# A product-key expert layer on one core: 640 dense and 384 gathered tokens instead of 704 and 320, and the second expert product turned round

## The chip, the cores and the metric

The kernel runs as one program on one core of a Trainium2 chip. The metric is the device time of one execution in microseconds (us). Three timed runs of the kernel before gave 2978.72, 2979.86 and 2987.46 us; their median, 2979.86 us, is what the change is compared with. Engines are named as in the profile: PE is TensorE, with PEld for its weight loads, DVE is VectorE, ACT is ScalarE, POOL is GpSimd and SP is SyncE. "Stage" below means a stretch of the program that is named by its place in time.

## The reference, cut to what matters

A sequence of 1024 tokens of width 1024 goes through a token-mixing half (norm, projections, a gated recurrence, a short convolution, an output projection, residual) and then through the half that the change touches, a layer of 16384 single-neuron experts (PEER):

```python
s = jnp.einsum('thpk,hpnk->thpn', q, sub_keys)          # 8 heads x 2 halves x 128 keys
top_s, top_i = lax.top_k(s, 16)
best_s, best_pos = lax.top_k(cand_s.reshape(T, 8, 256), 16)
gate = jax.nn.softmax(best_s, axis=-1)
u = expert_u[idx]                                        # 128 chosen experts of each token
v = expert_v[idx]
act = jax.nn.gelu(jnp.einsum('td,thkd->thk', xb, u))
return jnp.einsum('thk,thkd->td', gate * act, v)
```

After it come a gated residual and a final RMS norm. All is float32; the kernel reaches that precision on PE by splitting each operand into a high and a low part of fp32r and taking three products (high-high, high-low, low-high).

## The kernel before

**Two ways for the experts.** The tokens are divided. For the last `TD` = 704 ("dense") tokens the kernel computes all 16384 experts, in 128 blocks of 128: the first product (activations of a block for all dense tokens, `u_steps`, line L1161, 24 matmuls of 384 and 24 of 320 columns a block), a gelu, a multiplication with the block's gates, which are zero where an expert was not chosen (`w_step`, L1376), and the second product with the block's rows of v (`v_phase`, L1395). For the first `REST` = 320 ("gathered") tokens it fetches the 128 chosen rows of u and of v of each token by indirect DMA from POOL (L1082) and works on them on DVE: one multiply-and-sum per row of u (L1100) and one multiply-add per row of v (L1092). One such step handles one row for each of 128 tokens, a transfer of 128 x 4 KB. Two tiles of 128 tokens take 128 steps each, the half tile of 64 tokens takes 64 steps, with half of each token's experts on either half of the partitions and a small product that folds them: 320 steps of a row of u and a row of v.

**The stages in time.** Up to about 350 us: modulation, norm 1 and the mixing of the first half of the sequence. 350 to 420: queries and scores of the gathered tokens. 420 to 690: mixing of the second half, output projection, norm 2. 690 to 838: queries, scores and first top-k of the dense tokens (`query`, L873; `top16`, L922 to L926). 838 to 980: second top-k and index picking for the dense tokens. 980 to 1256: the dense gates (`gates`), for a group of 64 tokens at a time: DVE builds one-hot products (L1312, L1318), PE multiplies them (L1327), ACT copies the result (L1330), and SP stores 4 MB of gates in pieces of 512 bytes (L1335). 1256 to 2960: the main loop over 128 blocks. After that the end: transposing, residual, final norm, store.

**What runs beside it.** Forty blocks' activations (`EARLIES`) are computed ahead (`u_early`), strewn over the second top-k and the gates, and wait in DRAM (`ged`). The work on the gathered tokens is a generator, `background()`: top-k of each tile, then the rows. `advance(cost)` moves it on by a number of VectorE microseconds; the stages call it at rates of their own (`RATES`): 0.15 in the second mixing, 0.1 in the two stages of the dense top-k ("E"), 0.0 in the gates ("F"), 0.5 for the early blocks that remain after them ("G"), and evenly in the main loop, so that it ends at 97% of TensorE's columns (`along`, `per_column`). A planner orders the instructions of each engine: one whose inputs are ready can be put ahead of earlier program order. The row operations L1100 and L1092 are exempt from that (`keep_in_program_order`): each stands behind what was traced on DVE just before it. Rows are received in four buffers (`ROWS`) and one more. SP issues the loads of u (`wl`), of v (`vl`), of gates (`gsb`) and of early blocks, and the stores, in one queue; POOL issues the gathers in another.

**The second product.** Blocks are taken in groups of `SB` = 3. For each of the two column groups of tokens and each of eight slices of 128 output columns, v's slice is stationary and the weighted activations W (128 experts by 384 or 320 tokens) move: 9 matmuls into one PSUM bank. Two of the 16 results stay in PSUM for the whole loop (`FIXED`); the other 14 are added to accumulators in SBUF by DVE (L1411). The results are transposed, so the end of the kernel turns them back with 96 small products (L1424, L1425) before the final norm.

Of the kernel before, what the change touches and what calls it, by code (L numbers as in the profile page):

```python
# [32 lines left out]
TD = 704  # L33
REST = S - TD
SPL = [(0, 384), (384, TD - 384)]
# [4 lines left out]
# the gathered tokens of the last, half tile get their experts together with the half tile of the others  # L40
FULL = REST // P
LAST = REST % P
assert LAST and LAST == P - TD % P
SB = 3
# [18 lines left out]
FIXED = [(0, 0), (1, 0)]  # L63
# [17 lines left out]
RF = 0.0  # L81
# [16 lines left out]
def build(tc, A, out, dbg=None):  # L98
# [27 lines left out]
    def rsqrt(r, v, tmp, e=0):  # L126
        """of v / 4 ** e: a first guess from the exponent, then Newton steps"""
# [12 lines left out]
    with root:  # L140
# [6 lines left out]
        qgd = scratch.tile([16, P, LAST], F32, name="qgd")  # L147
# [29 lines left out]
        # ---------------------------------------------------------------- stationary operands  # L177
        # all of [P, KC, P], in the order in which TensorE takes them; each is fetched two and split one ahead
# [24 lines left out]
        def halve(n):  # L203
            """there is a third set of halves at times"""
# [7 lines left out]
        def deepen(pl, first, n, every):  # L212
            """that many more from the first on: one of so many goes into a pool of its own"""
# [18 lines left out]
        def ahead():  # L232
            """in the midst of the products with one: split the next"""
# [5 lines left out]
        # ---------------------------------------------------------------- constants, modulation  # L239
# [4 lines left out]
        # three buffers of four row tiles, in turn of the normalised input or w_out, and of the mix or the residual  # L244
# [36 lines left out]
        # TensorE gets to its full clock while the first loads are under way  # L281
# [29 lines left out]
        def mod_part(sec, wa, d):  # L311
            """some columns of a section of the modulation"""
# [5 lines left out]
        def mod_part_rows(sec, wa, d):  # L318
            """the same on TensorE, as a row that is turned into columns"""
# [28 lines left out]
        # ---------------------------------------------------------------- norm 1 and the values  # L348
# [14 lines left out]
        def lnT1(xs, pl, k, h1, onact=False):  # L363
            """transpose a column block of the four row tiles, scale, shift and split it"""
# [16 lines left out]
        def wi_load(pl, k, lb=3, hb=2, ahead=0, wait=[]):  # L381
            """loads run ahead of the splits"""
# [34 lines left out]
        # ---------------------------------------------------------------- projections, token mixing  # L417
# [6 lines left out]
        # lower bounds  # L424
# [16 lines left out]
        # a window of 32 columns of it holds ones in one of them  # L441
# [12 lines left out]
        def mixing(half, mods, h1, og):  # L454
            """projections, recurrence, convolution and group norms of half a sequence, into og"""
# [43 lines left out]
            # blocks of w_in: per head f, q, g (0..11), per conv group c, x, b (12..23)  # L499
# [54 lines left out]
            # masks of the levels: the highest bit in which s and t differ, for s < t  # L554
# [117 lines left out]
            def finish(g):  # L672
                """the scales of a group, from the rows of all of them"""
# [18 lines left out]
        # ---------------------------------------------------------------- w_out, norm 2  # L692
# [169 lines left out]
        def query(pl, hp, hs, spl, tiles, new_pq, new_sc, sink, n):  # L862
# [3 lines left out]
            if n > TD:  # L866
                SY.dma_start(qT[:, TD:], qgd[hp])
# [665 lines left out]
```

## Time and profile before

| | before |
|---|---|
| median of three timed runs | 2979.86 us |
| span of the profiled execution | 2982.4 us |
| PE busy | 2902.0 us (97%) |
| PE weight loads busy | 2750.8 us (92%) |
| DVE busy | 2524.2 us (85%) |
| ACT busy | 946.0 us (32%) |
| POOL busy | 796.2 us (27%) |
| moved by DMA | 709.65 MB, 238 GB/s over the span |

The profile is of one execution, whose first to last instruction took 2982.4 us. No other duration of that execution is on record; its span lies 2.5 us above the median of the timed runs and within their range. A busy share is an average over stages with different limits, so the windows by stage say more than the table. PE's busy time is modelled from pipelined matmuls: the time from one start to the next is what a matmul costs, not its listed duration. DVE's listed durations overlap in the same way by some 80 ns.

### The profile page before, as it was taken

The numbers are of one execution on the slowest core, as the hardware profiler recorded it, in microseconds if no ns is written. First come the engines' busy times: TensorE is split into PE (matmuls) and PEld (weight loads), VectorE is DVE, ScalarE is ACT, GpSimd is POOL, SyncE is SP. The second block draws the span as 40 slices with busy tenths as digits, with TensorE's granted clock in tenths as the row PEclk, the third lists the DMA queues.
The fourth block names the chain that finished last, engine by engine and source line by source line (L and its number), as shares of the span: only waits on it lengthen the run. The fifth ranks groups of instructions, "written<-read, shape, count | busy, mean of one in ns | idle before, by whom it ended". The sixth has DMA issues, their size and how long they took to land.

```text
span 2982.4 us, 47131 instructions
## 1 busy us (share of the span) xinstructions
PE 2902.0 (97%) x18242; PEld 2750.8 (92%) x18242; DVE 2524.2 (85%) x5314; ACT 946.0 (32%) x1541; POOL 796.2 (27%) x661
## 2 busy tenths in 40 slices
PE   8999999999999999999999999999999999999998
PEld 6887888878999899999999999999999999999997
DVE  6885559988999877568889989889989988989987
ACT  5643655433122444422222222222222221222221
POOL 0000000000000000015454445435545444444450
PEclk8999999989999999999999999999999999999999
DMA  7424342244223577778889888889889888889883
GB/s 269 146 88 142 130 142 71 85 146 147 61 89 108 181 238 241 234 257 299 302 305 335 314 309 327 320 304 336 304 306 325 319 317 318 307 318 332 304 311 128
DMA packets 286898, 709.65 MB, mean 238 GB/s; under 512 B 26513, under 2 KB 124817, under 8 KB 284370
## 3 DMA queue, kind: packets, MB, share of 16 engines
q1 hardware_dynamic: 192994, 365.56, 35.5%
q0 software_dynamic: 93680, 341.09, 32.2%
q8 instruction: 142, 2.33, 0.3%
q14 instruction: 82, 0.67, 0.1%
HBM read 633.65 MB, written 72.88 MB: 237 GB/s over the span
## 4 chain that ended last, share of the span: by engine, by line
PE 64%; DVE 17%; DMA 10%; issue 5%; ACT 2%; POOL 1%; SPq 0%; DVEq 0%; ACTq 0%; POOLq 0%
PE pv L1395 22%; PE pa L1161 19%; PE pp L467 6%; DMA wl<-in_uT 5%; PE pq L873 4%; PE pacc L1395 3%; DVE wl L114 2%; DMA Wl<-ged 2%; PE ps L577 1%; PE pp L873 1%; PE pg L1327 1%; PE pp L378 1%; DVE gacc L1092 1%; PE pp L714 1%; DVE acc L1411 1%
## 5 line engine op out<-in xcount | busy, mean ns | idle before, releaser
L1161 PE MATMUL pa<-h2h,wh 128*128 128x384 f32 (+1 forms) x1840 | 598.4, 325 | 2.7 <-ACT ge L1166 2.6
L1161 PE MATMUL pa<-h2h,wl 128*128 128x384 f32 (+1 forms) x1840 | 593.9, 323 | 0.0
L1161 PE MATMUL pa<-h2l,wh 128*128 128x384 f32 (+1 forms) x1840 | 593.7, 323 | 0.0
L1395 PE MATMUL pv<-Wh,vh 128*128 128x384 f32 (+1 forms) x1792 | 580.6, 324 | 11.7 <-DVE acc L1411 11.1
L1395 PE MATMUL pv<-Wl,vh 128*128 128x384 f32 (+1 forms) x1792 | 577.3, 322 | 0.0
L1395 PE MATMUL pv<-Wh,vl 128*128 128x384 f32 (+1 forms) x1792 | 577.0, 322 | 0.0
L1395 PEld LDWEIGHTS pv<-Wh,vh 128*128 128x128 f32 x1792 | 336.9, 188 | 22.4 <-DVE acc L1411 19.6
L1161 PEld LDWEIGHTS pa<-h2h,wh 128*128 128x128 f32 x1840 | 346.0, 188 | 4.5 <-ACT ge L1166 3.8
L1161 PEld LDWEIGHTS pa<-h2l,wh 128*128 128x128 f32 x1840 | 346.2, 188 | 0.0
L1161 PEld LDWEIGHTS pa<-h2h,wl 128*128 128x128 f32 x1840 | 346.0, 188 | 0.3 <-DVE wl L114 0.3
L113 ACT ACTIVATE Wh<-Wl 128x704 fp32r<-128x704 f32 x128 | 101.6, 793 | 747.8 <-PE pv L1395 588.2
L1395 PEld LDWEIGHTS pv<-Wh,vl 128*128 128x128 f32 x1792 | 337.0, 188 | 0.0
L1395 PEld LDWEIGHTS pv<-Wl,vh 128*128 128x128 f32 x1792 | 336.9, 188 | 0.0
L113 ACT ACTIVATE wh<-wl 128x1024 fp32r<-128x1024 f32 x187 | 198.0, 1059 | 420.8 <-DMA wl<-in_uT 205.2
L114 DVE TENSOR_TENSOR wl<-wl,wh 128x1024 fp32r<-128x1024 f32 x187 | 227.8, 1218 | 97.7 <-ACT wh L113 95.9
L1411 DVE TENSOR_TENSOR acc<-acc,pv 128x320 f32<-128x320 f32 (+1 forms) x574 | 286.1, 513 | 11.6 <-PE pv L1395 11.3
L114 DVE TENSOR_TENSOR vl<-vl,vh 128x1024 fp32r<-128x1024 f32 x128 | 156.0, 1219 | 18.3 <-ACT vh L113 18.2
L113 ACT ACTIVATE vh<-vl 128x1024 fp32r<-128x1024 f32 x128 | 134.6, 1052 | 79.5 <-DMA vl<-in_v 45.4
L467 PE MATMUL pp<-h1h,wh 128*128 128x512 f32 x384 | 156.6, 408 | 0.0
L467 PE MATMUL pp<-h1h,wl 128*128 128x512 f32 x384 | 152.5, 397 | 3.5 <-DVE wl L114 3.4
L1376 DVE TENSOR_TENSOR Wl<-Wl,gsb 128x704 f32<-128x704 f32 x128 | 113.2, 885 | 48.4 <-DMA Wl<-ged 36.9
L467 PE MATMUL pp<-h1l,wh 128*128 128x512 f32 x384 | 152.3, 397 | 0.0
(1778 smaller groups left out, 5978.2 us busy)
## 6 DMA issues: line engine op xcount, KB each, us to landing
wl<-in_uT SPq DMA_DIRECT2D x128, 512.0 KB
vl<-in_v SPq DMA_DIRECT2D x128, 512.0 KB
gd<-stg SPq DMA_DIRECT2D x11, 4096.0 KB
gsb<-gd SPq DMA_DIRECT2D x64, 704.0 KB
wl<-in_win SPq DMA_DIRECT2D x48, 512.0 KB
wa<-in_wada SPq DMA_DIRECT2D x16, 1024.0 KB
wl<-in_wq SPq DMA_DIRECT2D x32, 512.0 KB
ged<-ge SPq DMA_DIRECT2D x40, 352.0 KB
```

The lines of the kernel that those rows point to most:

```text
L113: C.activation(hi, src, AF.Copy)
L114: V.tensor_tensor(lo, src, hi.bitcast(F32), op=OP.subtract)
L378: T.matmul(pvs[t], l[:, t * P:(t + 1) * P], r, start=(k == 0 and l is h1[0][k] and r is wi[0]), stop=(k == KC - 1 and l is h1[1][k]))
L467: T.matmul(pp, l[:, k], r[k], start=(i == 0), stop=(i == 3 * KC - 1))
L577: T.matmul(ps_[:, c], X[:, cs_], Y[:, cs_], start=True, stop=True)
L714: T.matmul(pm, l[:, t * P:(t + 1) * P], r, start=(k == 0 and l is yh[k] and r is woh[k]), stop=(k == KC - 1 and l is yl[k]))
L873: T.matmul(pq[:, :m], l[:, k], hs[k, r][:, o:o + m], start=(i == 0), stop=(i == 3 * KC - 1))
L1092: V.scalar_tensor_tensor(ac, r, aw[:, j:j + 1], ac, op0=OP.mult, op1=OP.add))
L1161: T.matmul(pa[:, :n], l[:, k], h2[k, r][:, o:o + n], start=(i == 0), stop=(i == 3 * KC - 1))
L1376: V.tensor_tensor(gv, gv, gs[b // GB][:, :, b % GB], op=OP.mult)
L1395: T.matmul(pv[:, :n], l[:, c * P:(c + 1) * P], r[:, o:o + n], start=(i == 0 and (not fx or b0 == 0)), stop=(i == 3 * (b1 - b0) - 1 and (no ...
L1411: V.tensor_tensor(a, a, pv[:, :n], op=OP.add)
```

## The change

The dense tokens become 640 (five full tiles instead of five and a half) and the gathered ones 384 (three full tiles), so that the half tile, its fold and its round trip through DRAM are gone. The first product has two column groups of 320. The gates have ten groups of 64 tokens instead of eleven. In the second product the roles are exchanged: W's 128 tokens are stationary, 512 columns of v move, and the result of a tile of 128 tokens is 128 x 1024 in two PSUM banks, in token rows. Groups are of four blocks. One tile's sum stays in PSUM; the other four are added to SBUF accumulators of 128 x 1024. The end needs no transposing: a multiplication with a row of gate2, an addition and the norm. The background's rate in the gates goes from 0.0 to 0.9. The scores of the gathered tokens are stored two at a time instead of four. Comments are taken out as well.

```diff
-TD = 704
+TD = 640
-SPL = [(0, 384), (384, TD - 384)]
+SPL = [(0, 320), (320, 320)]
-SB = 3
+SB = 4
-FIXED = [(0, 0), (1, 0)]
+FIXED = 0
-RF = 0.0
+RF = 0.9
...
-        accs = {(j, c): mp.tile([P, n], F32, name=f"acc{j}{c}") for j, (_, n) in enumerate(SPL) for c in range(KC)
-                if (j, c) not in FIXED}
-        fixed = {f: psM.tile([P, 512], F32, name=f"pacc{f[0]}{f[1]}", bufs=1) for f in FIXED}
+        accs = {t: mp.tile([P, DM], F32, name=f"acc{t}") for t in range(DT) if t != FIXED}
+        fixed = psM.tile([P, DM], F32, name="pacc", bufs=1)
-        work = 3.0 * KC * TD * (2 * NK - len(EARLIES)) * SPREAD
+        work = 3.0 * (KC * TD * (NK - len(EARLIES)) + DM * DT * NK) * SPREAD
...
         def v_phase(b0, b1):
             last = b1 == NK
-            for j, (o, n) in enumerate(SPL):
-                for c in range(KC):
-                    fx = (j, c) in fixed
-                    pv = fixed[j, c] if fx else new_pv()
+            for t in range(DT):
+                fx = t == FIXED
+                pv = fixed if fx else psM.tile([P, DM], F32, name="pv", bufs=2)
+                for j in range(2):
                     i = 0
                     for b in range(b0, b1):
                         wh, wl = Ws[b]
                         vh, vl = Vs[b]
-                        for l, r in ((vh, wh), (vl, wh), (vh, wl)):
-                            T.matmul(pv[:, :n], l[:, c * P:(c + 1) * P], r[:, o:o + n],
+                        for l, r in ((wh, vh), (wh, vl), (wl, vh)):
+                            T.matmul(pv[:, j * 512:(j + 1) * 512], l[:, t * P:(t + 1) * P], r[:, j * 512:(j + 1) * 512],
...
+                    if not last:
+                        along(3.0 * (b1 - b0) * 512)
+                if last:
+                    a = x1s[t] if fx else accs[t]
+                    V.tensor_tensor(rs[t], pv, g2, op=OP.mult)
+                    V.tensor_tensor(rs[t], rs[t], a, op=OP.add)
+                    norm_store(mp, REST + t * P, P, [rs[t][:, :512], rs[t][:, 512:]], fw, rs[t], sq)
+                elif not fx:
+                    a = accs[t]
+                    if b0 == 0:
+                        V.tensor_copy(a, pv)
                     else:
-                        V.tensor_tensor(a, a, pv[:, :n], op=OP.add)
...
+                        V.tensor_tensor(a, a, pv, op=OP.add)
```

## Rows read from the trace of the kernel before

**Rows 1.** The page of the profile: the span, the busy times of two engines, the chain of waits by engine, and the two DMA queues (packets, MB, time of their packets as a share of 16 engines' span; q0 is POOL's queue, q1 SP's).

```profile
span 2982.4 us, 47131 instructions
PE 2902.0 (97%) x18242; PEld 2750.8 (92%) x18242; DVE 2524.2 (85%) x5314; ACT 946.0 (32%) x1541; POOL 796.2 (27%) x661
...
q1 hardware_dynamic: 192994, 365.56, 35.5%
q0 software_dynamic: 93680, 341.09, 32.2%
...
PE 64%; DVE 17%; DMA 10%; issue 5%; ACT 2%; POOL 1%; SPq 0%; DVEq 0%; ACTq 0%; POOLq 0%
```

**Rows 2.** Busy time of each engine by stage. Columns: stretch, its length, busy us (instructions) of PE, PEld, DVE, ACT and POOL, the granted TensorE clock, the mean busy share of the 16 DMA engines, GB/s.

```profile
350.00:420.00 70.00, 67.53 (x462) 65.19 (x461) 23.43 (x25) 31.67 (x73) 1.59 (x3) 1.00 0.51 167
420.00:690.00 270.00, 251.83 (x1278) 207.00 (x1278) 247.33 (x852) 126.47 (x215) 9.47 (x11) 0.95 0.32 107
690.00:838.00 148.00, 148.00 (x970) 146.76 (x969) 138.60 (x749) 31.62 (x55) 0.00 (x0) 1.00 0.27 90
838.00:980.00 142.00, 133.81 (x807) 130.58 (x806) 138.04 (x611) 36.77 (x56) 0.76 (x1) 0.98 0.31 103
980.00:1256.00 276.00, 265.51 (x2486) 248.44 (x2487) 212.53 (x366) 136.16 (x254) 0.00 (x0) 0.99 0.74 226
1256.00:1283.00 27.00, 26.22 (x165) 25.88 (x164) 4.55 (x5) 6.04 (x9) 0.00 (x0) 1.00 0.95 312
1283.00:2960.00 1677.00, 1663.07 (x10300) 1649.33 (x10298) 1495.01 (x2129) 392.98 (x549) 781.08 (x634) 1.00 0.85 307
2960.00:2983.00 23.00, 13.38 (x97) 10.25 (x96) 13.32 (x49) 4.12 (x12) 0.00 (x0) 0.82 0.29 107
```

**Rows 3.** The same view of the steady part of the main loop alone.

```profile
1300.00:2900.00 1600.00, 1587.42 (x9841) 1576.90 (x9840) 1434.60 (x2012) 370.99 (x509) 773.21 (x628) 1.00 0.87 314
```

**Rows 4.** The chain of waits in order of time: start, us, what, and how many matmuls in a row. The L1395 pieces are of 320 columns (9.24) and of 384 (10.92), L1161 alternates 24 of each, L467 has 512 columns.

```profile
99.42 5.58 PE pp L467 x24
...
1021.32 18.62 DMA wl<-in_uT
...
1315.34 15.40 PE pa L1161 x96
...
1344.56 9.24 PE pv L1395 x63
...
1370.80 10.92 PE pv L1395 x63
```

**Rows 5.** The first product (L1161) alone by stretch: length, busy us (matmuls) of PE and (weight loads) of PEld, clock, DMA. A block has 48 matmuls.

```profile
838.00:980.00 142.00, 132.66 (x792) 129.22 (x792) 0.98 0.31 103
980.00:1256.00 276.00, 197.39 (x1063) 169.73 (x1064) 0.99 0.74 226
1256.00:2960.00 1704.00, 695.20 (x4291) 689.38 (x4289) 1.00 0.86 307
```

**Rows 6.** Waits in the main loop (1283 to 2960 us): who waited for whom, us in total, times, longest.

```profile
POOL more L1082 <- DVE gacc L1092: 76.9, 53, 9.6
...
PEld pv L1395 <- DVE acc L1411: 19.6, 30, 2.4
...
DVE more L1100 <- DMA more<-in_u,idx: 7.1, 4, 2.9
```

**Rows 7.** Instructions of DVE in order of time, in the main loop: start, us, what. Successive starts show what each costs when they follow one another.

```profile
1703.19 1.28 DVE L1092 SCALAR_TENSOR_TENSOR gacc<-grow__17319,aw,gacc 128x1024 f32<-128x1024 f32 x1
1704.38 0.48 DVE L1411 TENSOR_TENSOR acc<-acc,pv 128x320 f32<-128x320 f32 x1
...
1705.61 1.22 DVE L1100 SCALAR_TENSOR_TENSOR grow__17344<-grow__17344,hx 128x1024 f32<-128x1024 f32 x1
...
1706.75 0.48 DVE L1411 TENSOR_TENSOR acc<-acc,pv 128x320 f32<-128x320 f32 x1
1707.15 0.18 DVE L1109 TENSOR_TENSOR aw<-aw,gkg 128x32 f32<-128x32 f32 x1
...
1710.39 0.88 DVE L114 TENSOR_TENSOR Wl<-Wl,Wh 128x704 fp32r<-128x704 f32 x1
1711.19 1.22 DVE L114 TENSOR_TENSOR vl<-vl,vh 128x1024 fp32r<-128x1024 f32 x1
1712.33 1.28 DVE L1092 SCALAR_TENSOR_TENSOR gacc<-grow__17429,aw,gacc 128x1024 f32<-128x1024 f32 x1
```

**Rows 8.** Groups of instructions with their shapes: count, busy us, mean ns, idle before. The two forms of L1411 in the main loop, and the gates' matmul from 980 to 1256 us.

```profile
L1411 DVE TENSOR_TENSOR acc<-acc,pv 128x384 f32<-128x384 f32 x287 | 153.0, 545 | 0.2 <-PE pv L1395 0.2
L1411 DVE TENSOR_TENSOR acc<-acc,pv 128x320 f32<-128x320 f32 x287 | 133.2, 480 | 11.5 <-PE pv L1395 11.1
L1327 PE MATMUL pg<-O,P 128*128 128x128 f16 x1408 | 101.7, 219 | 9.9 <-DVE P L1318 9.4
```

**Rows 9.** One of the five operations of the top-k (L922) by stretch: length, busy us (instructions) of DVE, clock, DMA. A tile of 128 tokens has 24. The first two stretches are of gathered tiles.

```profile
420.00:545.00 125.00, 5.97 (x24) 0.99 0.25 82
545.00:650.00 105.00, 5.75 (x24) 0.92 0.33 109
650.00:690.00 40.00, 0.00 (x0) 0.89 0.50 177
690.00:900.00 210.00, 36.14 (x144) 0.98 0.27 91
```

More of the change, by code (lines that the diff above doesn't have):

```diff
@@ L41 @@
 FULL = REST // P
-LAST = REST % P
-assert LAST and LAST == P - TD % P
-SB = 3
+assert REST % P == 0 and TD % P == 0
+SB = 4
 GB = 2
@@ L890, in query @@
             scores.append(score)
-            return qT
         keysT = [None]
@@ L902, in sink_gather @@
         def sink_gather(hp, g, w, sc):
-            if hp % 4 == 0 and g == 0:
-                sgs[0] = qg.tile([P, FULL, 4, P], F32, name="sg", bufs=2)
+            if hp % 2 == 0 and g == 0:
+                sgs[0] = qg.tile([P, FULL, 2, P], F32, name="sg", bufs=2)
             s_ = sgs[0]
-            C.activation(s_[:w, g, hp % 4], sc, AF.Copy)
-            if hp % 4 == 3:
+            C.activation(s_[:w, g, hp % 2], sc, AF.Copy)
+            if hp % 2:
                 o = GG[g][0]
-                SY.dma_start(scd[o:o + w, hp - 3:hp + 1], s_[:w, g])
+                SY.dma_start(scd[o:o + w, hp - 1:hp + 1], s_[:w, g])
         for hp in range(16):
-            qT = query(qg, hp, hg2, [(0, REST)], GG[:FULL], lambda: bank("pp"), lambda: bank("ps"), sink_gather, REST)
-            SY.dma_start(qgd[hp], qT[:, FULL * P:])
+            query(qg, hp, hg2, [(0, REST)], GG, lambda: bank("pp"), lambda: bank("ps"), sink_gather, REST)
         scores.pop()()
@@ L1110, in background @@
                 parts = [ac[:, :512], ac[:, 512:]]
-                if c_ > 1:
-                    fold = gp.tile([P, P], F32, name="fold", bufs=1)[:, :w]
-                    V.tensor_copy(fold, ident[:, :w])
-                    for c in range(1, c_):
-                        V.tensor_tensor(fold, fold, ident[:, c * w:(c + 1) * w], op=OP.add)
-                    for j in range(2):
-                        pf = foldps[0]()[:w]
-                        T.matmul(pf, fold, parts[j], start=True, stop=True)
-                        parts[j] = pf
                 x1 = gp.tile([P, DM], F32, name="hx", bufs=1)
@@ L1204, in sink_dense @@
             top16(qp, sc, P, ts[:w, t, hp], ti[:w, t, hp])
-        foldps[0] = lambda: psE.tile([P, 512], F32, name="pq", bufs=3)
         for hp in range(16):
@@ L1236, in build @@
             early_along(pick(new, [a[:, t] for a in ab], ti[:, t], [i1[:, t], i2[:, t]]))
-        lo_, hi_ = slice(0, LAST), slice(P - LAST, P)
-        n = steps[FULL]
-        sl = slice(sum(steps[:FULL]), sum(steps))
-        i1f, i2f, gkf = (a[hi_, DT - 1].rearrange("p k h -> p (k h)") for a in (i1, i2, gk))
-        ih = qp.tile([P, P], I32, name="ih")[hi_]
-        V.scalar_tensor_tensor(ih, i1f, float(NK), i2f, op0=OP.mult, op1=OP.add)
-        SY.dma_start(idx[lo_, sl], ih[:, :n])
-        SY.dma_start(gkg[lo_, sl], gkf[:, :n])
-        V.tensor_copy(idx[hi_, sl], ih[:, n:])
-        V.tensor_copy(gkg[hi_, sl], gkf[:, n:])
         stE.close()
@@ L1456, in build @@
             prev += SB
-        fw = grow() if NG else mp.tile([P, DM], F32, name="fw")
+        fw, g2 = grow(), grow()
         SY.dma_start(fw, bcast_rows(A["fnw"]))
+        SY.dma_start(g2, bcast_rows(g2d[0]))
         sq = mp.tile([P, DM], F32R, name="vh", bufs=SLOTS)[:, :512].bitcast(F32)
@@ L1462, in build @@
         for t in range(DT):
-            n = ("wl", "wh")[t % 2] if t < 5 else "vl"
-            x1 = (mp.tile([P, DM], F32R, name=n, bufs=VS) if n == "vl" else
-                  up.tile([P, KC, P], F32R, name=n, bufs={"wl": WL, "wh": 2}[n]))
-            x1 = (x1 if n == "vl" else x1.rearrange("p k e -> p (k e)")).bitcast(F32)
-            SY.dma_start(x1[:WT[t]], x1d[REST + t * P:REST + t * P + WT[t]])
-            x1s.append(x1)
-            if t < 3 and NG:
-                rs.append(grow())
-            elif t < 5 and NG:
-                rs.append(gp.tile([P, DM], F32, name=("hx", "gacc")[t - 3], bufs=1))
-            else:
-                rs.append(mp.tile([P, DM], F32R, name="vl", bufs=VS).bitcast(F32))
-        for c in range(KC):
-            for j, (o, n) in enumerate(SPL):
-                if (j, c) not in fixed:
-                    a = accs[j, c]
-                    V.tensor_scalar(a, a, modc[:, 5, c:c + 1], None, op0=OP.mult)
+            n = ("wl", "wh")[t % 2]
+            x1 = up.tile([P, KC, P], F32R, name=n, bufs={"wl": WL, "wh": 2}[n]).rearrange("p k e -> p (k e)").bitcast(F32)
+            SY.dma_start(x1, x1d[REST + t * P:REST + (t + 1) * P])
+            x1s.append(x1)
+            rs.append(grow() if t < 2 else gp.tile([P, DM], F32, name=("hx", "gacc", "more")[t - 2], bufs=1))
+        for t, a in accs.items():
+            V.tensor_tensor(a, a, g2, op=OP.mult)
+            V.tensor_tensor(a, a, x1s[t], op=OP.add)
         v_phase(prev, NK)
```

42 lines of the change are left out of this document (removed).

## The prediction

> **What bounds the kernel now.** I read the page first: PE is busy for 97% of the span and holds 64% of the chain of waits [rows 1]. Then the windows by stage, since that share is a mean over stages [rows 2]. In the main loop, 56% of the span, PE is busy 1663 of 1677 us, and two others are close: DVE 1495 us, and the DMA engines at 0.85, or 0.87 in its steady part [rows 2, 3]. In the gates PE is full as well: 1063 matmuls are 22.1 blocks of 7.68 us, 170 us, and the gates' own matmuls take 102, together 272 of 276 us [rows 5, 8]. From 690 to 980 us DVE is the full one, 276.6 of 290 us [rows 2]. So a saving on PE is worth its whole size in the main loop as long as DVE and DMA don't become the limit, and the change puts 64 more steps on just these two.
>
> **Second product.** The time of a matmul is read from pieces of the chain: 63 of 384 columns in 10.92 us, 173.3 ns each; 63 of 320 in 9.24, 146.7 ns; 24 of 512 in 5.58, 232.5 ns [rows 4]. A block costs 24 x (173.3 + 146.7) = 7.68 us now. Five tiles x two halves x three products make 30 of 512: 6.975 us. Over 128 blocks 983 becomes 893: -90. The slope from 320 to 384 columns (0.416 ns a column) would give 226.5 ns for 512, 870 in all; in proportion to 320 columns it would be 234.7 ns, 901. I take 232.5, which is measured at this width.
>
> **First product.** 48 matmuls of 146.7 ns are 7.04 us instead of 7.68, -0.64 a block. After the gates 4291 / 48 = 89.4 blocks remain [rows 5]; with five sixths of the 16.5 now done from 838 to 980 and 25 in the gates (below), about as many, 89.2, remain afterwards.
>
> **Main loop, from the gates' end to 2960.** Now 1704 us = 983 + 89.4 x 7.68 + 34 of waits. Afterwards 893 + 89.2 x 7.04 = 1521 plus waits.
> DVE: the accumulation. The two forms differ by 65 ns for 64 columns [rows 8], and one of 320 takes 0.40 us from start to start [rows 7]; one of 1024 is then 0.40 + 704 x 1.02 ns = 1.12 us. Four of them for four blocks replace 7 x (0.40 + 0.465) for three: 1.12 us a block instead of 2.02. The two W operations go from 0.80 (704 wide) to 0.73. A gathered row costs 1.14 (u) or 1.19 us (v), 1.165 on average; a split of 1024 1.14 [rows 7]. With 768 rows less 133 done by then, DVE has 128 x (1.12 + 1.46 + 1.14) + 89 x 1.14 + 635 x 1.165 = 1317 us, a share of 0.84, below today's 0.89.
> DMA: POOL's queue takes 32.2% of 2982.4 us of 16 engines for 341 MB, 2.82 us a MB, so 1.476 us for a row of 128 x 4 KB [rows 1]. In the steady part 0.87 x 1600 = 1392 us are used, 628 gathers take 927 of it [rows 3], and 465 remain for u, v and gates, 495 for the whole loop, some 485 with 640 tokens. Afterwards 635 x 1.476 + 485 = 1422 us, 0.91 of 1567.
> PE's waits on the accumulation, 19.6 us now [rows 6], should shrink, since a bank pair comes back only two tiles (11 us) later. A new one appears: groups of four end, in ten of 32 cases, just before a block computed early, so no first product lies between the last W and the second product. That chain is a gelu, 0.73, a copy on ACT and 0.73, at least 2.6 us: 26 us over ten groups, where the planner can put the next block's product ahead. I take 11 of it: 45 us of waits, 1567 in all, **-137**; bounds -170 (no waits above 12) and -70 (below).
>
> **Gates.** Ten groups instead of eleven. A group calls the background eight times for 8 x 0.107 x 0.9 units and runs early blocks with each: 4032 columns are asked for, five steps of 960 come, so 4800 / 2400 x 0.9 = 1.8 units. That is 20.6 units a group, and 2.5 blocks. Before the gates some 42 units are spent (23 in the second mixing, 19 in E), and the top-k of three tiles needs 102. So three groups issue top-k and seven issue rows: 144 units are 32 rows of u (1.14 each) and 46 pairs (2.34), 124 rows, 17.7 a group; nine more follow in the rest of the early blocks.
> What a group costs then: PE 2.5 x 7.04 + 128 x 72 ns = 26.8 us [rows 8]; DVE 212.5 / 11 = 19.3 now, 39.9 with 17.7 rows; DMA 0.74 x 276 / 11 = 18.6 now, 44.7 with the rows [rows 2]. The rows are pinned in DVE's order, so what is built for PE queues behind a row that is late, and SP's loads of u share the engines with POOL's gathers: the chain has 18.62 us of waiting for a load of u already [rows 4]. Seven groups therefore take between 39.9 and 44.7; I take the middle, 42.3, since no row shows gathers and gate stores together. Three groups take 26.8, plus what of the third tile's top-k doesn't fit. Two gathered tiles are done by 650 us [rows 9]; the third comes after that. Its price is that of a dense tile: (276.6 - 32.5 splits x 1.14) / 6 = 40 us of DVE, of which 3 x 7.5 are free beside PE; 18 remain. Sum 80 + 18 + 296 = 394 instead of 276: **+118**. Bounds: 268 (all rows beside PE), -8; and 458 (engines at 0.87), +182.
>
> **Dense queries and top-k (690 to 980).** DVE sets the pace: five sixths of 240, plus 30 splits, 234 / 0.954 = 245 instead of 290: **-45**; -3 if the third gathered tile falls here and not in the gates. The 64 columns less of a query (16 x 0.64 us on PE) lie beside that.
>
> **Small ones.** Queries of gathered tokens, 350 to 420, where PE is full [rows 2]: 384 columns instead of 320, 16 x 24 x 26.6 ns = **+10**. The end: 96 small products go, with most of the 13.4 us of PE in its 23 us; **-10**, at least 0. The fold, the two DRAM trips of the half tile (32 KB each) and the scores' smaller stores (eight more) lie beside PE: 0; POOL's gathers in the gates have only one another behind them.
>
> **Sum.** 10 - 45 + 118 - 137 - 10 = -64 from the profiled span: 2918; the median of the runs lies 2.5 below that span, so **2916 us**, 2.1% faster.
>
> **A rule that speaks against it.** The clock is granted at 0.99 in the gates and at 0.82 at the end, where PE is busy 13.4 of 23 us [rows 2]; its levels are 1.2 and 2.4 GHz. In seven groups PE would idle 15 of 42 us. The Trainium skill, in "TensorE: Matmul & The Clock Gate", Part 1, says that the slow clock is the default and only activity lifts it; the window at the end agrees.
>
> **Rivals.**
> 1. *The rows hide in the gates, or slip out of them.* For it: DVE has 23% and DMA 26% free there [rows 2]. Against: 20.6 us of rows don't fit into 5.8 us of a group. The gates take 268 (-126); if the rows only slip, the main loop has up to 183 us more DMA, 1605, over its 1567, and gives back about 60. 2916 - 66 = 2850. Chance 0.2.
> 2. *The DMA engines don't go above 0.87.* The longest stretch shows 0.87, short ones 0.95 [rows 2, 3]. Then the loop's 1422 us take 1634 (+67) and seven groups 360 (+64): 3047. It decides below 0.907; at 0.89 the loop takes 1598 and the gates 52 more, 2999, slower. Against: POOL waits for DVE's buffers (76.9 us) and DVE for rows only 7.1 [rows 6]. Chance 0.13.
> 3. *Uncovered groups.* Each of the ten also waits for up to five rows queued on DVE: 10 x (2.6 + 5.8) = 84 instead of 11: 2989, no change. For it: DVE is 84% full and in order. Against: the planner can fill. Chance 0.12.
> 4. *The clock.* If all seven groups ran at 1.2 GHz, PE would need 53.6 us for each, 11.3 more than 42.3: +79, 2995. That is the page's rule taken whole; rows 2 show 0.82, not 0.5, with a worse share. Chance 0.05.
>
> **How the numbers follow.** My case has 0.5, with 2870 to 2965 as its own range (gates 350 to 440). The range 2845 to 2990 takes in rival 1 and the near ends of 2 to 4. What can't be told from no change is within 0.3%, 9 us. Faster: 0.5 + 0.2 and a third of the other 0.3, 0.80; same 0.07, from rival 3; slower 0.13, from 2 and 4.
>
> **What would show it.** L1395 from start to start: 232 ns. The stretch of L1327: near 390 us with PE at about 70%, waits for rows or u, DMA above 0.9; near 268 would prove rival 1. Main loop: PE as full as today, L1411 at 1.2 us, DMA 0.91; waits of L1395 for Wh or Wl in every third group would be rival 3, idle PE with waits for gathers and DMA stuck at 0.87 rival 2. I am wrong altogether if the gates grow and the loop doesn't shrink by 100 us.

## The result: slower by 1.1%, and the profile after

The changed kernel takes 3011.11 us (median of four runs, 3005.47 to 3025.67), the kernel before 2980.39 us in the same comparison. The ratio is 1.0107, 95% interval 1.0078 to 1.0135: slower by about 1%, clear of the noise, where 2916 us, 2.1% faster, were forecast. The profiled execution spans 3003.7 us, 7.4 below the median.

First lines of the page of the changed kernel: span, busy time by engine, the two DMA queues (packets, MB, share of 16 engines' span) and the chain of waits by engine. They answer to [rows 1].

```profile
span 3003.7 us, 41769 instructions
...
PE 2747.7 (91%) x15683; PEld 2428.5 (81%) x15683; DVE 2534.7 (84%) x5007; ACT 928.4 (31%) x1529; POOL 1029.7 (34%) x789
...
q0 software_dynamic: 112176, 408.47, 38.0%
q1 hardware_dynamic: 182994, 356.09, 34.8%
...
PE 44%; DVE 22%; DMA 17%; issue 10%; ACT 5%; POOL 1%; SPq 1%; DVEq 0%; ACTq 0%; POOLq 0%
```

PE lost 154 us of busy time and 20 points of the chain of waits; DMA rose from 10% to 17% there. POOL's gathers carry 67 MB more in all. No engine has become the full one in PE's place.

Busy time of each engine by stage, changed kernel (length; busy us of PE, PEld, DVE, ACT, POOL; granted clock, DMA share, GB/s). It answers to [rows 2]. The gates are the fourth line and the main loop the fifth.

```profile
350.00:436.00 86.00, 81.14 (x493) 78.72 (x492) 23.33 (x23) 35.30 (x86) 1.58 (x3) 1.00 0.49 158
436.00:704.00 268.00, 251.78 (x1278) 206.18 (x1277) 260.27 (x970) 125.16 (x214) 3.38 (x6) 0.95 0.31 99
704.00:972.00 268.00, 253.15 (x1696) 248.89 (x1694) 259.75 (x1266) 67.43 (x112) 6.47 (x6) 0.97 0.34 110
972.00:1361.00 389.00, 286.41 (x2373) 260.73 (x2374) 333.50 (x532) 128.53 (x237) 160.65 (x122) 0.84 0.90 309
1361.00:2990.00 1629.00, 1543.31 (x8166) 1368.26 (x8163) 1396.96 (x1658) 390.94 (x564) 854.27 (x640) 0.98 0.90 321
2990.00:3004.00 14.00, 0.00 (x0) 0.00 (x0) 9.46 (x30) 1.44 (x4) 0.00 (x0) 0.65 0.37 150
```

The gates take 389 us instead of 276 and the main loop 1629 instead of 1704. So the loop gives back 75 of the 113 us that the gates cost, and 137 were forecast. The loop issues 640 gathers, hardly more than the 634 of the kernel before [rows 2]; the added rows lie in the gates (122). The gathered queries take 86 instead of 70 us, the dense queries and top-k 268 instead of 290, the end 14 instead of 23.

PE's waits in the main loop, changed kernel (who waited for whom, us, times, longest), as [rows 6] has them for the kernel before; and one piece of the chain of waits, with the count of matmuls in a row, as in [rows 4].

```profile
PE pacc L1360 <- ACT Wh L112: 55.1, 27, 4.5
PE pa L1145 <- ACT wh L112: 13.8, 1, 13.8
PE pa L1145 <- ACT Wl L1150: 6.0, 5, 1.9
```

```profile
1578.04 19.50 PE pv L1360 x86
```

86 matmuls of 512 columns in 19.50 us are 226.7 ns each. The second product so needs 128 x 30 x 226.7 ns = 870 us, and the 89.9 blocks of the first product that the loop still does (4316 matmuls) need 633: **PE's own work is 1504 us, and the loop is 125 us longer**. (Some 21 us of the 125 are about 120 matmuls that start twice as far apart as the others; most of the rest are waits such as the ones above.) In the kernel before, 34 of 1704 us were of this kind, beside 1670 of work. All that follows asks what the 125 us are. For each run below "over PE's own" is the loop less 1504 us, less 1213 where a third of the second product is left out, and 1534 for the old product.

### The profile page after: what moved, and what is told of

It reads as the page before. It is cut to its first block, busy times and chain, and to the rows that moved or that the text cites. A ratio compares the mean times of both kernels' runs of the same rounds, so it can differ in the third digit from the quotient of the medians.

```text
span 3003.7 us, 41769 instructions
## 1 busy us (share of the span) xinstructions
PE 2747.7 (91%) x15683; PEld 2428.5 (81%) x15683; DVE 2534.7 (84%) x5007; ACT 928.4 (31%) x1529; POOL 1029.7 (34%) x789
## 4 chain that ended last, share of the span: by engine, by line
PE 44%; DVE 22%; DMA 17%; issue 10%; ACT 5%; POOL 1%; SPq 1%; DVEq 0%; ACTq 0%; POOLq 0%
PE pv L1360 18%; PE pa L1145 9%; DMA wl<-in_uT 6%; PE pp L465 5%; PE pacc L1360 4%; DMA Wl<-ged 3%; DVE wl L113 3%; DMA vl<-in_v 3%; DVE gacc L1085 2%; ACT wh L112 1%; DVE s L918 1%; DVE Wl L1340 1%; PE pq L869 1%; PE ps L575 1%; PE pp L376 1%
## 5 line engine op out<-in xcount | busy, mean ns | idle before, releaser
L1145 PE MATMUL pa<-h2h,wh 128*128 128x320 f32 x1840 | 582.3, 316 | 63.2 <-ACT wh L112 31.5
L1145 PE MATMUL pa<-h2h,wl 128*128 128x320 f32 x1840 | 578.1, 315 | 7.5 <-DVE wl L113 7.5
L1145 PE MATMUL pa<-h2l,wh 128*128 128x320 f32 x1840 | 578.6, 314 | 0.0
L1360 PE MATMUL pv<-vh,Wh 128*128 128x512 f32 x1024 | 403.1, 394 | 8.4 <-DVE hx L1368 4.0
L1360 PE MATMUL pv<-vl,Wh 128*128 128x512 f32 x1024 | 401.6, 392 | 0.0
L1360 PE MATMUL pv<-vh,Wl 128*128 128x512 f32 x1024 | 399.8, 391 | 0.0
L1360 PEld LDWEIGHTS pv<-vh,Wh 128*128 128x128 f32 x1024 | 194.1, 190 | 50.6 <-DVE hx L1368 4.4
L1360 PEld LDWEIGHTS pv<-vl,Wh 128*128 128x128 f32 x1024 | 194.1, 190 | 40.6
L1360 PEld LDWEIGHTS pv<-vh,Wl 128*128 128x128 f32 x1024 | 193.2, 189 | 40.5
L1376 DVE TENSOR_TENSOR acc<-acc,pv 128x1024 f32<-128x1024 f32 x120 | 145.8, 1215 | 25.3 <-PE pv L1360 25.1
L1360 PE MATMUL pacc<-vh,Wh 128*128 128x512 f32 x256 | 108.1, 422 | 55.2 <-ACT Wh L112 55.1
```

Source lines behind the costliest of these rows:

```text
L1145: T.matmul(pa[:, :n], l[:, k], h2[k, r][:, o:o + n], start=(i == 0), stop=(i == 3 * KC - 1))
L1360: T.matmul(pv[:, j * 512:(j + 1) * 512], l[:, t * P:(t + 1) * P], r[:, j * 512:(j + 1) * 512], start=(i == 0 and (not fx or b0 == 0)), sto ...
L1376: V.tensor_tensor(a, a, pv, op=OP.add)
```

## Experiments

**Where the waits surface.** The first four runs start from the wait that the profile names: the second product waits for W. It could be the groups that end before an early block, W's buffers, the number of blocks in a group, or the rows that the gates take on.

```diff
 early4: -EARLIES = [b for b in range(NK) if b % 3 == 1][:EARLY]
         +EARLIES = [b for b in range(NK) if b % 4 == 2 or b % 16 == 1][:EARLY]
 sb3:    -SB = 4        +SB = 3
 ws2:    -WS = SLOTS + 2    +WS = SLOTS + 4
 rf0:    -RF = 0.9      +RF = 0.0
```

> The changed kernel with other blocks computed early: b % 4 == 2 (32) and b % 16 == 1 (8) instead of b % 3 == 1, still 40, so that neither a group's last block nor the block behind it, after which the second product stands, is ever an early one. Theory 1 (no first product lies between the group's last W and the second product, since every third group ends at an early block or is followed by one): the wait of the fixed bank's matmuls for Wh falls from 60 us over 27 groups to under 20, the main loop from 1629 to about 1585, the whole to about 2965. Theory 2 (loads of early activations and of u land late because DMA is at 0.91, wherever they stand): 50 us or more remain and the time is 3000 to 3020.

> The changed kernel with groups of three blocks instead of four (buffers follow, one fewer of each). The block after a group (3, 6, 9, ...) is never an early one. Theory 1 (uncovered groups): waits for Wh under 20 us, main loop about 1590 although DVE gets 4 x 11 more accumulations of 1.12 us (49 us, share 0.86 to 0.89); the whole 2965 to 2980. Theory 2 (late landing under DMA load): waits of 50 us or more remain, the whole 3005 to 3025. Theory 3 (too few W buffers for a group of four): as theory 1.

> The changed kernel with two more buffers for the low parts and raw values of W (9 instead of 7), groups of four as changed. Theory 3 (a group of four fills its buffers, so that the last W can't be prepared while the second product of the group before runs): waits for Wh fall from 60 to under 25 us, the whole to 2970 to 2985. Theories 1 and 2: the order of the work or the load of DMA decides, the waits stay at 45 to 65 us and the time within 8 us of 3011.

> The changed kernel with the background's rate in the gates back at 0.0; all else as changed (3011 us; gates 972 to 1361 us, DMA 0.94 busy from 1050 on). Theory (the 113 us that the gates grew are the gathered rows, about 137 of them, on full DMA engines): the gates shrink to 265 to 285 us, POOL is at 0 there, DMA falls to 0.75, the clock rises from 0.84 to 0.99. The rows, 1.476 us of 16 engines each, then lie in the main loop, which needs 0.90 x 1629 + 200 = 1666 us of DMA. If the loop's engines can run at 0.97 it takes about 1720 and the whole 2985 to 2995; if they stay at 0.91, 1830 and the whole is 3090. Rival (the gates grew for another reason, the clock or DVE): they stay above 340 us.

Measured: early4 3027.48 us, above both of its expectations (ratio to the kernel before 1.0175, 1.0150 to 1.0201), sb3 3018.46 (1.0145, 1.0117 to 1.0174), ws2 3022.78 (1.0165, 1.0130 to 1.0199), rf0 3099.35 (1.0420, 1.0399 to 1.0442). Their loops take 1646, 1626, 1639 and 1856 us. PE's longest wait in the loop of early4, and then in that of sb3:

```profile
PE pacc L1360 <- ACT Wh L112: 63.5, 24, 8.5
```

```profile
PE pv L1360 <- DVE acc L1376: 56.7, 28, 5.2
```

Without a single uncovered group the wait for W is as long as before, so my third rival falls. With groups of three it is gone (2.0 us), and a wait for the accumulation of the same size stands in its place: the loop is 122 us over PE's own instead of 125. More buffers for W bring nothing (ws2 came out 12 us above the changed kernel, not within the 8 expected). So the name in the wait view tells where a delay surfaces, not where it arises.

The windows of rf0, gates and loop, show the price of the rows. Without them the gates take 250 us, and the loop 227 more than in the changed kernel; together 2106 against 2018.

```profile
976.00:1226.00 250.00, 234.67 (x2254) 219.58 (x2255) 192.25 (x330) 122.10 (x227) 0.00 (x0) 0.97 0.74 221
1226.00:3082.00 1856.00, 1631.36 (x8261) 1421.98 (x8258) 1540.45 (x1852) 393.90 (x572) 1021.38 (x759) 0.94 0.88 316
```

**Which resource.** Next, one resource at a time is relieved: half of the gathers left out (halfdma), row operations on 128 columns (halfdve), two of the three products of the second product (pe23), one more row buffer (rows5).

```diff
 halfdma: +                    if taken_rows[0] % 2 == 0:
          +                        return last_row[0]
 halfdve: -V.scalar_tensor_tensor(r, r, 1.0, hx, ...
          +V.scalar_tensor_tensor(r[:, :128], r[:, :128], 1.0, hx[:, :128], ...
          ...   (the multiply-add of a row of v in the same way)
 pe23:    -for l, r in ((wh, vh), (wh, vl), (wl, vh)):
          +for l, r in ((wh, vh), (wh, vl)):
 rows5:   -ROWS = 4      +ROWS = 5
```

> The changed kernel with every second gather left out: the row operation on VectorE that belonged to it works on the row fetched before, so VectorE's work is as it was and POOL's queue moves half. What it leaves out: half of the fetched expert rows of the 384 gathered tokens. Theory D (the DMA engines, stuck at 0.90 to 0.91, are what the main loop and the gates wait for; the waits of PE for W or for the accumulation are where it shows): DMA need of the main loop falls from 1466 to about 1000 us, PE's 1504 us become the limit: main loop 1535 to 1560 instead of 1629, gates 300 to 365, the whole 2860 to 2930. Theory V (VectorE, 0.86 busy and in order, is the limit): main loop above 1600, the whole above 2960.

> The changed kernel with all gathers, but the two row operations on VectorE work on 128 of the 1024 columns. What it leaves out: seven eighths of the arithmetic on the fetched rows. Theory D: the same bytes move, so the main loop stays at 1595 to 1630 and the gates at 370 to 390; the whole 2960 to 3010. Theory V: about 0.9 us less for each of 768 rows; main loop 1540 or less, gates 300 or less, the whole 2830 to 2870.

> The changed kernel with two of the three products in the second expert product (the low part of W is not multiplied). What it leaves out: one of three partial products of v. TensorE's work in the main loop falls by 290 us, from 1504 to 1214. Theory D: the loop keeps to the DMA engines and stays at 1560 to 1620, the whole 2940 to 3000. Rival P (TensorE is still the limit and its waits come on top): the loop falls to 1330 to 1400, the whole to 2710 to 2780.

> The changed kernel with five buffers and one more for fetched rows instead of four and one more. Gathers land 6.4 us after issue (median) and one is taken every 2.5 us. Theory D (the engines' rate decides): no change, 3000 to 3020. Theory L (the landing time with five buffers decides): main loop 40 us or more shorter, the whole 2960 or less.

Measured: halfdma 2901.31 us (0.9740, 0.9713 to 0.9768), halfdve 3010.96 (1.0109, 1.0081 to 1.0136), pe23 3008.21 (1.0099, 1.0074 to 1.0125), rows5 3016.72 (1.0121, 1.0101 to 1.0142). The main loops of halfdma, halfdve and pe23:

```profile
1323.00:2889.00 1566.00, 1524.24 (x8157) 1359.18 (x8156) 1393.35 (x1655) 389.92 (x563) 467.29 (x318) 0.99 0.68 225
```

```profile
1337.00:3000.00 1663.00, 1564.01 (x8255) 1386.65 (x8253) 818.48 (x1676) 393.83 (x571) 670.27 (x651) 0.97 0.87 319
```

```profile
1368.00:2993.00 1625.00, 1336.59 (x6877) 1171.86 (x6876) 1384.35 (x1643) 385.67 (x560) 871.26 (x640) 0.91 0.89 321
```

290 us of matmuls less take 4 us off the loop, and 580 us of DVE work less take nothing off it (its gates end 24 us sooner and leave it more of the first product). Half of the gathers less take off 63 us, with the row operations still in place. Up to here "the DMA engines have a ceiling at about 0.91" (theory D of the expectations) explained which runs gain and which don't, though not every size: the loops of halfdma, halfdve and pe23 lie 6, 33 and 5 us above what it had stated. So I took bytes off the other queue.

**Bytes of SP's queue.** The gates are stored and loaded as 16-bit floats, four blocks to a load instead of two, in the changed kernel and in the kernel before; each gate is rounded to 11 bits by that.

```diff
-GB = 2
+GB = 4
-gd = scratch.tile([NK // GB, P, NTG, GB, TG], F32, name="gd")
+gd = scratch.tile([NK // GB, P, NTG, GB, TG], F16, name="gd")
...
```

> The changed kernel with the dense gates stored and loaded as 16-bit floats (four blocks to a load, so that the pieces stay at 512 bytes). The gates lose the bits behind the eleventh; every engine's instructions stay as they are, and so do the gathers. SP's queue moves 21 MB less in the gates and 21 MB less in the main loop; at its 1045 us of 16 engines for 356 MB (2.94 us a MB) that is 62 us of DMA engines in each. Theory D (the bytes on the DMA engines bound both stages): the main loop falls from 1629 to PE's own limit, about 1567 as in the run with half the gathers, the gates from 389 to about 355; 2890 to 2945 us in all. Theory of POOL's queue (the gathers' own issue and landing set the pace, SP's bytes don't matter): 3000 to 3020, as the gathers are unchanged. Theory of the engines' order (PE, ACT and DVE waiting on one another): 3000 to 3020 as well.

> The kernel before with the same edit: gates stored and loaded as 16-bit floats, the rest as it was. Theory D: its main loop runs with the DMA engines at 0.85 and PE at 0.99, its gates with PE at 0.96, so 42 MB less bring nothing: 2965 to 2985 us, and the DMA share of the loop falls to about 0.82. If fewer bytes also shorten PE's waits there, that is, if any byte less helps: 2930 to 2950 in the kernel before too, and the gain in the changed kernel says nothing about a bound.

Measured: after16 2957.22 us (0.9919, 0.9888 to 0.9951), before16 2952.26 (0.9903, 0.9875 to 0.9931). They lie 0.8% and 1.0% below the kernel before. Gates and loop of after16, then of before16:

```profile
979.00:1325.00 346.00, 284.50 (x2379) 256.73 (x2379) 333.36 (x532) 128.04 (x239) 162.42 (x123) 0.88 0.85 293
1325.00:2942.00 1617.00, 1540.61 (x8156) 1368.58 (x8156) 1394.16 (x1658) 390.38 (x563) 856.74 (x640) 0.98 0.88 309
```

```profile
980.00:1240.00 260.00, 259.22 (x2475) 244.54 (x2474) 211.23 (x358) 136.14 (x251) 0.00 (x0) 1.00 0.51 157
1240.00:2926.00 1686.00, 1681.87 (x10464) 1674.53 (x10462) 1503.24 (x2135) 398.89 (x558) 771.83 (x634) 1.00 0.85 295
```

The gates do what theory D said (346 us instead of 389). The loop doesn't: it lost 12 us, not 62, and stays 113 over PE's own with the DMA engines at 0.88. And the kernel before gained 28 us where theory D gave it none. A ceiling of the DMA engines at 0.91 isn't what holds the loop.

**Bytes of which queue.** Two runs take bytes away in different places: half rows in every gather (halfbytes), and the block of v loaded once (vonce).

```diff
 halfbytes: -G.indirect_dma_start(out=r, out_offset=None, in_=src,
            +G.indirect_dma_start(out=r[:, 512:], out_offset=None, in_=src.rearrange("a (b c) -> (a b) c", c=512),
            ...   (DVE reads the half that has come twice)
 vonce:     -            SY.dma_start(raw, A["v"][b * P:(b + 1) * P])
            +            if b == 0:
            +                SY.dma_start(Vs["raw"], A["v"][:P])
            ...
```

> The changed kernel with every gather in place, but of half rows (128 x 2 KB instead of 128 x 4 KB); DVE works on the full 1024 columns by reading the half that has come twice. Left out: the other half of each chosen row. Bytes theory (what counts is how long the DMA engines are kept, whoever asks): 201 MB less, as in the run with half the gathers, 2885 to 2925 us, loop 1560 to 1590. Theory of the gathers (their number, issue and landing count): 3000 to 3020, loop near 1629.

> The changed kernel with the block of v loaded once and split again for each block: SP moves 67 MB less, all of it in the main loop, and no split of v waits for a load; the splits and products stay. Left out: 127 of the 128 blocks of v. Bytes theory: 67 x 2.94 = 197 us of DMA engines less, the loop falls to 1560 to 1590 and the time to 2940 to 2975. Theory of the gathers: 2995 to 3020, since they are untouched. Between the two (2975 to 2995): the loads' own landing, not the engines' load.

Measured: halfbytes 2901.35 us (0.9732, 0.9713 to 0.9750), vonce 2993.14 (1.0042, 1.0027 to 1.0057). Their loops:

```profile
1326.00:2888.00 1562.00, 1525.62 (x8158) 1359.81 (x8156) 1391.14 (x1656) 390.64 (x564) 872.54 (x640) 0.99 0.69 227
```

```profile
1367.00:2971.00 1604.00, 1536.08 (x8162) 1364.25 (x8159) 1391.66 (x1658) 388.09 (x564) 874.25 (x640) 0.98 0.83 284
```

640 gathers of 2 KB rows are as good as 318 of 4 KB: the number of gathers doesn't count, their bytes do, or the packets, of which either run moves half as many on POOL's queue. 67 MB less on SP's queue take 25 us off the loop (18 off the median of the whole, whose runs spread over 22), at a DMA share of 0.83, below the kernel before. That run lies between the two theories, where the expectation had put the loads' own landing.

**Two resources at a time.** The last three runs relieve a second resource on top of the first: two of three products in the run with v loaded once (vonce_pe23) and in the run with half rows (halfbytes_pe23), and row operations on 128 columns in the first (vonce_halfdve). The edits are the ones shown above, combined.

> The run with v loaded once, and with two of the three products of the second product (128 x 10 x 226.7 ns = 290 us of PE less). Left out: 127 blocks of v and the low part of W. Its loop was 1604 us with all products. Theory of the gathers' own pace (640 whole rows at 2.51 us): the loop stays at 1580 to 1604. Theory of near-full resources that hold one another up, PE among them: 1430 to 1540, since PE needs 1213 us and DVE some 1400.

> The run with half rows in every gather, and with two of the three products of the second product (290 us of PE less). Left out: half of each chosen row and the low part of W. Its loop was 1562 us with all products, 58 over PE's own 1504. If PE sets that loop: 1400 to 1500 us, down to what DVE's row and split work allows (about 1390 busy). If DVE's order sets it: 1540 to 1562.

> The run with v loaded once, and with row operations on 128 of the 1024 columns, so that DVE has some 580 us less to do in the loop. Left out: 127 blocks of v and 896 columns of each row. Theory of the gathers' own pace: the loop stays near 1604. Theory of resources that hold one another up, DVE among them: it falls to PE's own 1504 plus some 50, 1550 to 1575.

Measured: vonce_pe23 2991.83 us (1.0043, 1.0021 to 1.0064), halfbytes_pe23 2796.26 (0.9394, 0.9367 to 0.9422), vonce_halfdve 3019.57 (1.0133, 1.0102 to 1.0164). The loops in that order:

```profile
1367.00:2977.00 1610.00, 1339.36 (x6878) 1173.12 (x6876) 1381.59 (x1647) 384.13 (x560) 895.00 (x640) 0.92 0.82 283
```

```profile
1325.00:2784.00 1459.00, 1289.51 (x6877) 1147.48 (x6876) 1377.79 (x1647) 387.99 (x560) 887.17 (x640) 0.94 0.73 242
```

```profile
1338.00:3005.00 1667.00, 1565.62 (x8258) 1387.98 (x8255) 817.82 (x1674) 391.63 (x570) 685.85 (x652) 0.97 0.78 278
```

With all rows whole the loop stays at 1604 to 1667 us whatever is taken from PE or DVE, even at a DMA share of 0.78. (vonce_halfdve's 1667 lies 63 us above the highest that either theory gave it; 14 of them are two blocks of the first product that its shorter gates leave, the rest isn't explained.) With half rows PE limits: 290 us of matmuls less take 103 us off, until DVE is busy 1378 of 1459 us. With PE out of the way the two queues are told apart: against pe23 (1625), 168 MB less of the loop's gathers (640 x 128 x 2 KB) take 166 us off, 1 us a MB, and 67 MB less of v 15 us, 0.2 us a MB. (In the changed kernel itself the two differ less: 67 us for 168 MB, where PE's own work cuts the gain short, and 25 for 67.) So only lighter gathers free the loop. That isn't a fixed pace of whole rows, though: in their steady parts the run without rows in the gates (rf0, first line) takes 623 of them in 1400 us, one in 2.25, and the changed kernel (second line) 568, one in 2.46, with the DMA engines at 0.91 in both.

```profile
1450.00:2850.00 1400.00, 1216.27 (x6063) 1054.20 (x6062) 1196.51 (x1428) 285.99 (x408) 838.24 (x623) 0.94 0.91 328
```

```profile
1450.00:2850.00 1400.00, 1339.62 (x7076) 1186.16 (x7075) 1209.85 (x1425) 337.05 (x476) 758.02 (x568) 0.98 0.91 324
```

In some of the runs the loop goes with how soon a row lands, worked out from the trace's packet records (a gather's packets counted off in order, from the end of its POOL instruction to the end of the last packet; medians from 1450 to 2850 us, or to 2700 where the loop ends sooner): 4.2 us in the changed kernel, 4.0 with 16-bit gates, 3.7 with v loaded once, 2.4 with half rows, with loops of 1629, 1617, 1604 and 1562. Two runs stand outside this order: half the gathers (3.3 us, 1566), which needs only half as many rows, and vonce_halfdve (4.2 us, 1667). So this is a correlation and no cause.

**The product by itself.** The old second product is put into the changed kernel, in groups of four blocks (oldprod) and of three (oldprod3).

```diff
-for l, r in ((wh, vh), (wh, vl), (wl, vh)):
-    T.matmul(pv[:, j * 512:(j + 1) * 512], l[:, t * P:(t + 1) * P], r[:, j * 512:(j + 1) * 512],
+for l, r in ((vh, wh), (vl, wh), (vh, wl)):
+    T.matmul(pv[:, :n], l[:, c * P:(c + 1) * P], r[:, o:o + n],
...
```

> The changed kernel with the second product turned back: v's slices stationary, W's 320 columns moving, 16 results of 320 columns in groups of four blocks, 14 of them added to accumulators by DVE; the rest (640 and 384 tokens, rates, gates) as in the changed kernel. Left out: turning the sums back at the end, so the rows stored are not the layer's. PE gets 48 x 146.7 = 7.04 us a block instead of 30 x 226.9 = 6.81, 30 us more in the loop; DVE gets 14 x 0.40 for four blocks instead of 4 x 1.12, about 36 us more. Theory D: nothing of both is seen, 3000 to 3025 us, main loop 1620 to 1640. Theory of PE: 3035 to 3050. Theory of DVE: 3040 to 3055.

> The run with the old product (v stationary, 16 results of 320 columns), now in groups of three blocks as in the kernel before; the rest as in the changed kernel. Left out: turning the sums back at the end. PE has 30 us more than in the changed kernel, DVE 14 x 0.40 for three blocks instead of 4 x 1.12 for four, 96 us more in the loop. If groups of four made the old product slow (four blocks of v held for 28 us): 3010 to 3045 us. If the product itself does (more DVE work in an order that already fills): 3090 to 3130.

Measured: oldprod 3103.61 us (1.0409, 1.0379 to 1.0439), oldprod3 3041.69 (1.0200, 1.0179 to 1.0221). The loops of oldprod and oldprod3:

```profile
1363.00:3094.00 1731.00, 1594.90 (x10460) 1577.12 (x10460) 1439.45 (x2024) 391.83 (x566) 770.83 (x640) 0.96 0.86 303
```

```profile
1371.00:3028.00 1657.00, 1576.31 (x10465) 1553.88 (x10462) 1479.94 (x2160) 389.43 (x564) 761.95 (x640) 0.98 0.89 316
```

oldprod came out 49 us above the highest of its expectations; by the second run its excess belongs to groups of four, which the old product bears badly (197 us over PE's own, 123 with groups of three). Between oldprod3 and the changed kernel lie 30.6 us, and 28 of them in the loop. That is as much as the turned product's PE saving, 1534 - 1504, with the waits unchanged; it could also be part of the 96 us of DVE work that it saves. These runs don't tell the two apart, and pe23 and halfdve, where far larger savings on either brought nothing, show that neither can be counted on alone. With groups of three on both sides (sb3 and oldprod3) the turned product is 23 us ahead. The rest of the change, the division into 640 and 384 tokens with the rows in the gates, costs 61 us: 3041.69 against 2980, though the turning at the end is left out.

## Why the prediction was wrong

*Second product.* 226.7 ns, not 232.5: the slope that I had set aside (226.5) was right, and the loop's own PE work came out at 1504 instead of 1521 us.

*First product and the gathers left for the loop.* 89.9 blocks for 89.2, 640 gathers for 635. Right.

*The loop's waits: the step that failed.* "1521 plus waits", with 45 us of waits, was to make 1567. It has 125 over PE's own. The whole miss of the loop is there: 80 us more waits, 17 us less work. I worked out the DMA share (0.91 of 1567 us, measured 0.90 of 1629) and then gave it no price in the sum, because the share was below one. With half rows the loop takes 1562 us: the forecast holds, waits included (58), once the rows carry half their bytes. So 67 of the 125 us hang on the bytes of the gathers, and the sum had no term for them. They aren't due to more rows in the loop (640 gathers, 634 before): nearly the same rows had to pass beside 166 us less of PE's work, and PE's waits grew from 34 to 125. That saving PE "is worth its whole size as long as DVE and DMA don't become the limit" is a condition that I read from busy shares, and they don't show it: the changed kernel is held at 0.90, and vonce_halfdve at 0.78. My share for DVE, 0.84 "below today's 0.89", wasn't like for like either: the first counts from start to start, the second adds up listed durations. Listed, DVE is busy 1397 us, which would have been 0.89 of 1567; halfdve shows that this isn't what costs the time.

*Gates.* +113 against +118, but the near hit is luck, since two misses cancel. The first three groups, without rows, took 63 us instead of 98, as the third tile's top-k had been done before them and 4.5 early blocks came with them instead of 7.5; the seven with rows took 326 instead of 296, that is 46.6 us each, above both of my bounds (39.9 for DVE, 44.7 for the DMA engines). The next two lines are these two parts.

```profile
972.00:1035.00 63.00, 59.56 (x606) 54.52 (x606) 58.01 (x107) 34.33 (x65) 0.00 (x0) 0.97 0.66 204
1035.00:1361.00 326.00, 226.85 (x1767) 206.21 (x1768) 275.49 (x426) 94.21 (x172) 160.65 (x122) 0.81 0.95 329
```

The DMA engines are at 0.95 in the second part, and fewer bytes on either queue shorten it: with 21 MB less stored (after16, first line) it takes 287 us, with half rows (halfbytes, second line) 289, near what I had given DVE alone, 7 x 39.9 = 279.

```profile
1038.00:1325.00 287.00, 225.89 (x1770) 203.30 (x1770) 274.83 (x425) 94.20 (x174) 161.60 (x123) 0.85 0.93 324
```

```profile
1037.00:1326.00 289.00, 222.91 (x1773) 202.55 (x1773) 275.02 (x426) 94.44 (x173) 165.38 (x122) 0.86 0.83 264
```

*Dense queries and top-k.* -22 against -45, inside the bounds. The reason is the one named there, the third gathered tile: DVE is busy 260 us here, and 234 were counted for the dense tiles and the splits. L916 answers to L922 in [rows 9]: 24 of these a tile, 120 for five dense ones, and 9 more here; the tile's other 15 came before.

```profile
436.00:704.00 268.00, 16.06 (x64) 0.95 0.31 99
704.00:830.00 126.00, 18.74 (x71) 0.95 0.29 97
830.00:972.00 142.00, 12.21 (x58) 0.99 0.39 120
```

*Small ones.* Gathered queries +16 (10), the end -9 (-10). The span came out 86 us above 2918: 62 from the loop, 23 from the dense top-k, the rest from these and the gates. The median adds ten, since it lies above the profiled span instead of 2.5 below.

*Rivals.* Rival 2 had the right side and nearly the right loop (1634; measured 1629), by the wrong mechanism: no ceiling at 0.87 or at 0.91 holds, since seven groups of the gates run at 0.95 and the loop of vonce is slow at 0.83. (Its gates at 0.89 were to take 52 us more; by its own numbers it is 55.) I gave it 0.13, against it the 76.9 us in which POOL waits for DVE's buffers. Rival 3 put its wait in the right place, L1360 behind Wh, and had the wrong cause. Rival 1 is refuted by 389 us of gates. Rival 4 happens in part: the clock is granted at 0.84 in the gates, where PE is busy 286 of 389 us, and at 0.97 in rf0, where it is busy 235 of 250. The rule of the Trainium skill ("TensorE: Matmul & The Clock Gate", Part 1), that only activity lifts the clock, agrees with these two rows. By the starts, some 320 matmuls of the changed kernel's gates came at twice their distance and cost about 25 us, where the rival gave 79.

**What stays open.** Shown is that fewer bytes in the gathers shorten the loop, by 67 us, or by 166 with PE out of the way, where a MB of SP's queue brings a fifth as much; and that the gathers' number, one more row buffer, and PE's or DVE's work alone don't. Why the loop doesn't run faster with whole rows isn't shown: a row keeps the 16 engines for 1.48 us and the loop takes one in 2.5, while rf0 has taken one in 2.25. A row's buffer is bound to DVE's order until its operation has run, so a late landing could hold up what is queued behind it (the splits, W) and, through it, PE. The trace of halfdve points that way: with its row work cut, DVE is idle for 841 us of the loop, and 263 of these end with the landing of a row; in the changed kernel it is 55 of 227. No run tests it, as only one more buffer was tried.

## What to carry to other kernels

A share of 0.9 on a shared resource isn't "not the limit": before PE's saving is booked, ask whether the same transfers can pass in the shorter time, and price their waits, even where each engine has room. The name in a wait view is where delay surfaces; before mending it, relieve one resource at a time and see which one moves the stage, and then a second on top. A change in two parts is to be priced in two parts: here the turned product brought 23 to 31 us, and the new division of the tokens cost 61. And a sum that comes out right is to be checked term by term, as the gates show.

## What the runs showed of the hardware

A matmul of 512 columns of v took 226.7 ns from start to start, while the one of [rows 4] on the same width (L467) took 232.5. Halving the rows of a gather (4 to 2 KB) took its landing from 4.2 to 2.4 us, while 67 MB less on the other queue took it only to 3.7. And bytes cost time where the DMA engines have room: 46 MB less made the kernel before 28 us faster, with PE busy for 96% of its gates and 99% of its loop, and the DMA engines at 0.74 and 0.86.
